# A hybrid GLA and mLSTM block on one core: TensorE's order in the heads written out by stages

## The chip, the core and the metric

The kernel runs on one core of a Trainium2 chip. The metric is the device time of one execution in microseconds (us). A core has five engines that run beside each other and are kept in step by semaphores: TensorE (PE in the profile; matrix products, with PEld for loading their weights), VectorE (DVE), ScalarE (ACT), GpSimd (POOL) and SyncE (SP, which issues the DMAs here). Each engine executes its own list of instructions in order.

## The reference

One layer of a backbone block: 512 latent tokens and 256 context tokens of width 2048, all in float32. After an RMSNorm with a shift and a scale, one input projection feeds two groups of four heads each. The first four heads are gated linear attention (GLA) with a decay for each channel, the last four are mLSTM with an exponential input gate. Each head has keys and queries of 128 and values of 256, runs in both directions, and each latent scan starts from the final context state of its direction.

```
rel = where(tril, bcum[j] - bcum[i], -inf)              # GLA, bcum = cumsum(log decay)
scores = einsum('jk,ik,jik->ji', q, k, exp(rel))
o = scores @ v + (q * exp(bcum)) @ s                    # s: state so far
s_new = exp(b_end) * s + (k * exp(b_end - bcum)).T @ v
```

Head outputs are normalised, gated and multiplied by an output matrix; then come a second RMSNorm, a SwiGLU mixer of width 5504 with a 3x3 depthwise convolution, and a final RMSNorm.

## The kernel before

Tiles have 128 partitions. Activations are kept transposed, the width in 16 tiles of 128 x 512. A product with float32 weights is made as three products of a faster format: each weight chunk is split into a high part (a cast on ScalarE, L89) and a low part (a subtraction on VectorE, L90), and mm3 multiplies high by high, high by low and low by high (all these products show as L95). `load_split` loads a chunk of two 128-row blocks through SP, splits it with high priority, and also takes `rate` items from a list of fillers: chunks of the modulation product, which are summed on VectorE, ScalarE and GpSimd (L228 to L235) and closed by small TensorE products.

The order of the work. Instructions are traced in Python, and a planner orders each engine's list by priority (order of tracing, with blocks raised by `high_priority`) and by its own estimate of when operands are ready. Instructions marked with `keep_in_program_order` stay in traced order among each other. `mm` does so while `pinned[0]` is set, which is the case in `project_first` alone, the stage ahead of the heads. In the heads TensorE's order is thus the planner's.

The heads. `project(h)` makes the products of head h into six PSUM banks (q, k, two of v, and two of the context's k and v), in eight chunks of six groups. `evict` copies them out (ScalarE and VectorE). Head 1's sums are made early, together with head 0's, so that head 1 needs no projection of its own. PSUM has six banks for projections and two (`psb`) for all the rest.

`gla` (heads 0 to 3) makes, in this order: the context's decays (cdec, a log-sigmoid of three ScalarE steps and one on VectorE, csum by triangles of ones, kd, and the context's state cst); the latent decays (dec, log-sigmoid, a scan bt for each direction at L589, and b2, the same across blocks, L593 and L596); the scores sd of a token with itself; nine levels, with blocks of 1 to 256 tokens; qi; the output products po (L662); and `finish`, which normalises and transposes (yt). In a level with block b, the decays of the tokens relative to the edge between two neighbour blocks are formed. GpSimd subtracts for the one side (L617, L618), VectorE for the other (L80), ScalarE takes the exponential of all (L621), VectorE multiplies by q and k (L83), TensorE multiplies (sl, L631 and L643), and VectorE copies the result under a mask (L634). The tile ex of a level has two buffers.

`ml_gates` is traced ahead of head 4 and makes the mLSTM gates for all heads: small products pre, a log-sigmoid, two scans for each direction, and transposes pa of the results. `mlstm` (heads 4 to 7) makes the context's state (kt, cst), exponentials of gate differences (pg, qs, ed, with a triangular mask on GpSimd), scores s, outputs po and `finish`. After the heads come the gate projections (ga), the output projection (wo) and the mixer.

Of the kernel before, what the change touches and what calls it, by code (L numbers as in the profile page):

```python
# [18 lines left out]
P = 128  # L19
# [50 lines left out]
def block_kernel(ctx: ExitStack, tc: tile.TileContext, a: dict, out: bass.AP):  # L70
# [27 lines left out]

    def mm3(o, ah, al, bh, bl, start, stop, **kw):
# [69 lines left out]
    def unit(src, name, xh, xl, n=4):  # L169

        accs = [acc(f"{name}_{i}") for i in range(n)]
# [111 lines left out]
    def project(h):  # L283

        banks = [acc(f"a{h}_{g}", BANKS[g]) for g in range(6)]
# [243 lines left out]
    def finish(h, ob, ssq, yT):  # L529

        var = wtile(f"var{h}", "st1", TJ)
        scr = wtile(f"scr{h}", "st2", TJ)
        r = wtile(f"rs{h}", "st3", TJ)
        mean_eps(var, ssq, DV)
        rsqrt(var, scr, r)
        for j in range(TJ):
            V.tensor_scalar(out=ob[:, j, :], in0=ob[:, j, :], scalar1=r[:, j : j + 1], scalar2=None, op0=ALU.mult)
        for b in range(2):
            ps = psb(f"yt{h}_{b}")
            for j in range(TJ):  # L540
                PE.transpose(ps[:, P * j : P * j + P], ob[:, j, P * b : P * b + P], ident)
# [4 lines left out]
    def gla(h, pair, qk, v, kn, vn, yT):  # L546
        wlr = wk.tile([17, 2, DK], F32, name=f"wlr{h}", tag="wlr")
        nc.sync.dma_start(wlr, a["w_lr"][h])

        cla = ytile(13, f"cla{h}", (P, 2, CJ, DK))  # L550
        ct = ytile(15, f"ct{h}", (P, 2, CJ, DK))
        for d in range(2):
            ps = psb(f"cdec{h}{d}", (P, CJ, DK))
            for j in range(CJ):
                PE.matmul(ps[:, j, :], glr[0:17, T + P * j : T + P * j + P], wlr[:, d, :], start=True, stop=True)
            log_sigmoid(cla[:, d], ps, ct[:, d])
        ps = psb(f"csum{h}", (P, 2, CJ, DK))
        for d in range(2):
            tri = cc(C_LS) if d == 0 else cc(C_US)
            for j in range(CJ):  # L560
                more = j == d
                PE.matmul(ps[:, d, j, :], tri, cla[:, d, j, :], start=True, stop=not more)
                if more:
                    PE.matmul(ps[:, d, j, :], ones, cla[:, d, 1 - j, :], start=False, stop=True)
        kd = ytile(14, f"kd{h}", (P, 2, CJ, DK))
        S.activation(kd, ps, AF.Exp, scale=DECAY)
        for j in range(CJ):
            mul(kd[:, :, j], kd[:, :, j], kn[j].unsqueeze(1).to_broadcast([P, 2, DK]))
        ps = psb(f"cst{h}", (P, 2, DV))
        for d in range(2):  # L570
            for j in range(CJ):
                PE.matmul(ps[:, d, :], kd[:, d, j, :], vn[j][:, 0:DV], start=(j == 0), stop=(j == CJ - 1))
        s0 = wtile(f"s0{h}", "state", 2, DV + 2)
        S.copy(s0[:, :, 0:DV], ps)

# [6 lines left out]
        for d in range(2):  # L582
            ps = psb(f"dec{h}{d}")
            PE.matmul(ps, wlr[:, d, :], glr[0:17, 0:T], start=True, stop=True)
# [4 lines left out]
            V.tensor_tensor_scan(out=o, data0=seg, data1=x, initial=0.0, op0=ALU.mult, op1=ALU.add)  # L589
        for d in range(2):  # L590
# [7 lines left out]


        sc = wtile(f"sc{h}", "la", 2, TJ, P)  # L600
        scd, sc1 = sc[:, 0], sc[:, 1]
        sc2 = [ytile(12 + i, f"sc2{h}{i}", (P, 2, 2 * P)) for i in range(2)]
        ps = psb(f"sd{h}", (P, TJ, P))
        for j in range(TJ):
            PE.matmul(ps[:, j, :], qk[1][:, P * j : P * j + P], qk[0][:, P * j : P * j + P], start=True, stop=True)
        V.scalar_tensor_tensor(out=scd, in0=ps, scalar=2.0, in1=ident.unsqueeze(1).to_broadcast([P, TJ, P]),
                               op0=ALU.mult, op1=ALU.mult)
        for lv, b in enumerate(LEVELS + [P, 2 * P]):
            src = bt if b < P else b2
            ex = wk2.tile([P, 2, T], F32, name=f"ex{h}_{lv}", tag="ex")  # L610
            e4 = ex.rearrange("p s (n a b) -> p s n a b", a=2, b=b)
            sf = src[0].rearrange("p (n a b) -> p n a b", a=2, b=b)
            sb = src[1].rearrange("p (n a b) -> p n a b", a=2, b=b)
            n = T // (2 * b)
            rf = sf[:, :, 0, b - 1 : b].to_broadcast([P, n, b])
            rb = sb[:, :, 1, 0:1].to_broadcast([P, n, b])
# [10 lines left out]
            if b <= P:  # L627
                ps = psb(f"sl{h}_{lv}", (P, TJ, P))
                for i in range(TJ):
                    j = i if b < P else i ^ 1  # L630
                    PE.matmul(ps[:, i, :], ex[:, 1, P * i : P * i + P], ex[:, 0, P * j : P * j + P],  # L631
                              start=True, stop=True)
# [4 lines left out]
            else:  # L637
                for half in range(2):
                    ps = psb(f"sl{h}_{lv}_{half}", (P, 2, 2 * P))
                    for ii in range(2):  # L640
                        i = 2 * half + ii
                        j0 = 2 * P * (1 - half)
                        PE.matmul(ps[:, ii, :], ex[:, 1, P * i : P * i + P], ex[:, 0, j0 : j0 + 2 * P],  # L643
                                  start=True, stop=True)
                    S.copy(sc2[half], ps)
        qi = wtile(f"qi{h}", "tmp", 2, T)
        for d in range(2):
            S.activation(qi[:, d, :], b2[d], AF.Exp, scale=DECAY)
        mul(qi, qi, qk[0].unsqueeze(1).to_broadcast([P, 2, T]))
# [3 lines left out]
        for j in range(TJ):  # L653
# [7 lines left out]
            for n, (l, r) in enumerate(parts):  # L661
                PE.matmul(po, l, r, start=(n == 0), stop=(n == len(parts) - 1))  # L662
            S.activation(junk, po, AF.Square, accum_out=ssq[:, j : j + 1])
            V.tensor_copy(ob[:, j, :], po)
        finish(h, ob, ssq, yT)

    def ml_gates():
# [11 lines left out]
        for t, r in ((0, li), (1, pf)):  # L679
            for c0, n, at in ((0, T, lat0), (T, TC, ctx0)):  # L680
                ps = psb(f"pre{t}{c0}", (36, n))
                for d in range(2):
                    e = C_ID + 32 + 8 * d + 4 * t
                    PE.matmul(ps[rows[d], :], cst[32:48, e : e + H], glr[32:48, c0 : c0 + n], start=True, stop=True)
# [16 lines left out]
        add(cum, cum, gmx)  # L701
        dg = wk.tile([36, H], F32, name="dg", tag="st1")
        for d in range(2):
            pa = psb(f"pa{d}", (P, CJ + 2 * TJ, H))
            e = cst[rows[d], C_ID + 32 * d : C_ID + 32 * d + H]
            for j in range(CJ + TJ):
                s = ctx0[d] + P * j if j < CJ else lat0[d] + P * (j - CJ)
                PE.transpose(pa[:, j, :], li[rows[d], s : s + P], e)
            for j in range(TJ):
                s = lat0[d] + P * j  # L710
                PE.transpose(pa[:, CJ + TJ + j, :], cum[rows[d], s : s + P], e)
# [7 lines left out]
            PE.matmul(pg, cst[rows[d], C_ONE : C_ONE + 1].to_broadcast([H, P]), dg[rows[d], :], start=True, stop=True)  # L719
            V.tensor_copy(gccol[:, d, :], pg)  # L720
        for d in range(2):
# [4 lines left out]
    def mlstm(h, _, qk, v, kn, vn, yT):  # L726
# [9 lines left out]
        for d in range(2):  # L736
            ps = psb(f"cst{h}{d}", (P, DV + 2))
            for j in range(CJ):
                PE.matmul(ps, kt[:, d, j, :], vn[j], start=(j == 0), stop=(j == CJ - 1))
            S.copy(c0[:, d, :], ps)  # L740

        qs = wtile(f"qs{h}", "tmp", 2, T)
        pd = []
        for d in range(2):
            rows = slice(32 * d, 32 * d + H)
            pg = psb(f"pg{h}{d}")
            PE.matmul(pg, cst[rows, C_ID + 32 * d + hh : C_ID + 32 * d + hh + 1].to_broadcast([H, P]), negg[rows, :],
# [16 lines left out]
            pd.append(spans)  # L764
        for i in range(TJ):
            ps = psb(f"s{h}{i}")
            PE.matmul(ps, k[:, P * i : P * i + P], q, start=True, stop=True)
            for d in range(2):
                e, j0, j1 = pd[d][i]
                mul(e, e, ps[:, j0:j1])  # L770
        ssq = wtile(f"ssq{h}", "ssq", TJ)
        junk = wtile(f"junk{h}", "kn", DV)
        ob = wtile(f"ob{h}", "la", TJ, DV)
        for j in range(TJ):
            for d in range(2):
                po = psb(f"po{h}_{j}{d}", (P, DV + 2))
                js = slice(P * j, P * j + P)
                PE.matmul(po, qs[:, d, js], c0[:, d, :], start=True, stop=False)
                rng = range(j + 1) if d == 0 else range(j, TJ)
                for i in rng:  # L780
                    e, j0, _ = pd[d][i]
                    PE.matmul(po, e[:, P * j - j0 : P * j - j0 + P], v[i], start=False, stop=(i == rng[-1]))  # L782
# [10 lines left out]
            S.activation(junk, ob[:, j, :], AF.Square, accum_out=ssq[:, j : j + 1])  # L793
        finish(h, ob, ssq, yT)

    yT = []
    mod_fillers((2, 3, 4), 3)
    for h in range(2 * H):
        if h == 1:
# [3 lines left out]
        else:  # L803
            tiles = evict(h, first if h == 0 else project(h))
        if h == H:
            ml_gates()
        (mlstm if h >= H else gla)(h, *tiles, yT)
# [8 lines left out]
    for g in range(4):  # L816
        accs = unit(a["w_gates"][g], f"ga{g}", *hx)
# [259 lines left out]
```

## Time and profile before

| what | value |
|---|---|
| median of 3 runs | 2632.07 us (2631.95 to 2634.08) |
| the profiled execution | 2632.04 us |
| its span in the trace | 2630.2 us |
| TensorE busy | 2557.7 us |
| the chain that ended last, TensorE's share | 85% |

The span runs from the first to the last instruction of the trace; 1.8 us of the execution lie around it. In the chain's list and the timelines, the columns are start, length and what ran; in the groups of instructions, busy time in us, mean length in ns, and the idle time of the engine ahead of them with what ended it. Products are pipelined, so a length of one product overlaps that of the next. The heads run from about 209 us to 836 us.

### The profile page before, as it was taken

To read this page: it belongs to the slowest core of one execution; us is meant where nothing else is said; L and a number is where in the kernel's file an instruction comes from. 1 tells how busy PE (TensorE), PEld (TensorE's weight loads), DVE (VectorE), ACT (ScalarE), POOL (GpSimd) and SP (SyncE) were. 2 spreads that over 40 slices of the span, in tenths; PEclk is the share of its full clock that TensorE was granted. 3 is DMA by queue.
4 is the path that set the end of the run, shared out by engine and by line. 5 is a ranking of instruction groups with operands and counts; after the bars stand their busy time and mean duration, and the time that the engine had idled before them with its cause. 6 is when DMAs were issued, how large, how long until landed. Compare 5 with 4: busy or idle time off the path is not lost.

```text
span 2630.2 us, 31995 instructions
## 1 busy us (share of the span) xinstructions
PE 2557.7 (97%) x12866; PEld 2137.8 (81%) x12866; DVE 1362.1 (52%) x1971; ACT 861.3 (33%) x1219; POOL 285.9 (11%) x255
## 2 busy tenths in 40 slices
PE   6999999899999999999999999999999999999998
PEld 4887888778987887887878888888888888888887
DVE  6656664654334455547676436543653365336534
ACT  4223443323333444334343223222322233223332
POOL 0002221302112232310231000000000000000001
PEclk9999999999999999999999999999999999999998
DMA  8750101213322566642554222222233223222333
GB/s 317 281 198 34 39 35 67 71 41 112 126 90 106 191 222 232 204 165 76 192 184 160 96 96 96 97 96 97 97 100 100 97 96 97 96 96 87 102 96 101
DMA packets 96348, 321.38 MB, mean 122 GB/s; under 512 B 10884, under 2 KB 15304, under 8 KB 96200
## 3 DMA queue, kind: packets, MB, share of 16 engines
q1 hardware_dynamic: 96200, 319.34, 35.2%
q8 instruction: 101, 1.65, 0.3%
q14 instruction: 47, 0.39, 0.0%
HBM read 315.10 MB, written 4.19 MB: 121 GB/s over the span
## 4 chain that ended last, share of the span: by engine, by line
PE 85%; DVE 7%; DMA 3%; ACT 2%; issue 2%; POOL 0%; SPq 0%; POOLq 0%; ACTq 0%; DVEq 0%
PE ug L95 17%; PE dn L95 17%; PE uv L95 16%; PE a L95 14%; PE wo L95 6%; PE ga L95 5%; DMA raw_m<-in_w_mod 2%; PE po L662 2%; PE po L782 1%; PE ps_m L95 1%; PE sl L631 1%; DVE cv L924 1%; DVE ex L80 1%; PE dl L95 1%; DVE ex L83 1%
## 5 line engine op out<-in xcount | busy, mean ns | idle before, releaser
L95 PE MATMUL ug<-h2h,hi_ug 128*128 128x512 f32 x688 | 269.0, 392 | 1.6 <-ACT h2h L883 1.6
L95 PE MATMUL uv<-h2h,lo_uv 128*128 128x512 f32 x688 | 268.7, 391 | 1.4 <-DVE lo_uv L90 1.4
L95 PE MATMUL uv<-h2h,hi_uv 128*128 128x512 f32 x688 | 268.4, 390 | 1.4 <-ACT hi_uv L89 1.4
L95 PE MATMUL ug<-h2h,lo_ug 128*128 128x512 f32 x688 | 268.8, 391 | 0.2 <-DVE lo_ug L90 0.2
L95 PE MATMUL ug<-h2l,hi_ug 128*128 128x512 f32 x688 | 268.7, 391 | 0.0
L95 PE MATMUL uv<-h2l,hi_uv 128*128 128x512 f32 x688 | 268.4, 390 | 0.0
L95 PE MATMUL dn<-gh,hi_d 128*128 128x512 f32 x644 | 250.5, 389 | 0.0
L95 PE MATMUL dn<-gl,hi_d 128*128 128x512 f32 x644 | 250.5, 389 | 0.0
L95 PE MATMUL dn<-gh,lo_d 128*128 128x512 f32 x644 | 250.5, 389 | 0.0
L924 DVE SCALAR_TENSOR_TENSOR cv<-pad,cwt,cv 128x512 f32<-128x512 f32 x344 | 242.3, 759 | 10.6 <-ACT cv L922 9.1
L233 POOL TENSOR_TENSOR sum_m<-sum_m,raw_m 128x512 f32<-128x512 f32 x112 | 173.8, 1551 | 550.8 <-ACT raw_m L232 315.0
L90 DVE TENSOR_TENSOR lo_ug<-raw_ug,hi_ug 128x1024 fp32r<-128x1024 f32 (+1 forms) x88 | 106.8, 1214 | 243.0 <-ACT hi_ug L89 243.0
L90 DVE TENSOR_TENSOR lo_uv<-raw_uv,hi_uv 128x1024 fp32r<-128x1024 f32 (+1 forms) x88 | 105.3, 1197 | 181.1 <-ACT hi_uv L89 180.7
L90 DVE TENSOR_TENSOR lo_d<-raw_d,hi_d 128x1024 fp32r<-128x1024 f32 x82 | 98.7, 1204 | 165.5 <-ACT hi_d L89 164.6
L231 DVE SCALAR_TENSOR_TENSOR sum_m<-raw_m,csil,sum_m 128x512 f32<-128x512 f32 x112 | 101.0, 902 | 152.0 <-DMA raw_m<-in_w_mod 148.5
L89 ACT CAST hi_ug<-raw_ug 128x1024 fp32r<-128x1024 f32 (+1 forms) x88 | 90.8, 1032 | 269.6 <-PE ug L95 202.0
L89 ACT CAST hi_d<-raw_d 128x1024 fp32r<-128x1024 f32 x82 | 85.1, 1037 | 278.7 <-PE dn L95 224.4
L89 ACT CAST hi_uv<-raw_uv 128x1024 fp32r<-128x1024 f32 (+1 forms) x88 | 90.9, 1033 | 251.5 <-PE uv L95 181.0
L95 PEld LDWEIGHTS uv<-h2h,lo_uv 128*128 128x128 f32 x688 | 129.5, 188 | 29.7 <-DVE lo_uv L90 2.7
L95 PEld LDWEIGHTS ug<-h2h,hi_ug 128*128 128x128 f32 x688 | 129.8, 189 | 28.7 <-ACT h2h L883 1.9
L95 PEld LDWEIGHTS uv<-h2h,hi_uv 128*128 128x128 f32 x688 | 129.6, 188 | 28.5 <-ACT hi_uv L89 1.8
L95 PEld LDWEIGHTS ug<-h2h,lo_ug 128*128 128x128 f32 x688 | 129.7, 189 | 27.9 <-DVE lo_ug L90 0.6
(310 smaller groups left out, 5279.2 us busy)
## 6 DMA issues: line engine op xcount, KB each, us to landing
raw_m<-in_w_mod SPq DMA_DIRECT2D x192, 512.0 KB, 4.4
raw_ug<-in_w_up SPq DMA_DIRECT2D x80, 512.0 KB, 3.1
raw_uv<-in_w_up SPq DMA_DIRECT2D x80, 512.0 KB, 3.2
raw_d<-in_w_down SPq DMA_DIRECT2D x79, 512.0 KB, 3.3
raw_h<-in_w_heads SPq DMA_DIRECT2D x64, 512.0 KB, 3.2
raw_ga<-in_w_gates SPq DMA_DIRECT2D x32, 512.0 KB, 3.3
raw_wo<-in_w_out SPq DMA_DIRECT2D x32, 512.0 KB, 4.1
xl<-in_xT SPq DMA_DIRECT2D x16, 256.0 KB, 5.3
```

Of the source, the lines that this page charges most:

```text
L80: V.tensor_tensor(out=o, in0=x, in1=y, op=ALU.subtract)
L83: V.tensor_tensor(out=o, in0=x, in1=y, op=ALU.mult)
L89: S.copy(hi, x)
L90: return V.tensor_tensor(out=lo, in0=x, in1=hi.bitcast(F32), op=ALU.subtract).ins
L95: ins = PE.matmul(*args, **kw)
L231: V.scalar_tensor_tensor(out=dv, in0=raw[:, 0, :], scalar=ce, in1=dv, op0=ALU.mult, op1=ALU.add)
L233: G.tensor_tensor(out=po, in0=po, in1=raw[:, 1, :], op=ALU.add)
L631: PE.matmul(ps[:, i, :], ex[:, 1, P * i : P * i + P], ex[:, 0, P * j : P * j + P], start=True, stop=True)
L662: PE.matmul(po, l, r, start=(n == 0), stop=(n == len(parts) - 1))
L782: PE.matmul(po, e[:, P * j - j0 : P * j - j0 + P], v[i], start=False, stop=(i == rng[-1]))
L924: V.scalar_tensor_tensor(out=t3, in0=src, scalar=w, in1=t3, op0=ALU.mult, op1=ALU.add)
```

## The change

It makes three edits, all in the heads.

TensorE's order is written out. `pinned` is set for all of the heads, and every product and transpose of the stages goes through `mm` or `tr`. The projection becomes a generator that yields after each group with the group's length; the stages (`gla`, `gla_prep`, `ml_gates`, `mlstm`) become generators that yield how much of the projection is to stand behind what they have just traced; `weave` runs the two together. While heads 0 and 1 run, the projection of head 2 is the fill; for every later head it is the next head's, and in head 7 the first unit of the gate projections. What is left of the projection follows after the head's stages.

The decays are made early. `gla_prep` holds the dec, cdec and csum stages. Head 0's are traced ahead of head 0, those of head h + 1 between head h's output products and its `finish`. The state cst and qi move behind the third level. `ml_gates` is traced behind head 3's `finish`.

The levels' differences are made by VectorE alone, one instruction for each direction over 512 elements, which writes both halves of ex crosswise; the exponential becomes two instructions, for the two signs. In the levels of 128 and 256 the subtraction is gone: ScalarE takes it as a bias (`ends`), in 8 and 4 instructions.

```diff
+    def weave(stages, steps):
+        debt = 0.0
+        for need in stages:
+            debt += need
+            while debt > 0:
+                took = next(steps, None)
+                if took is None:
+                    debt = 0.0
+                    break
+                debt -= took
...
+    def project_steps(h, banks):
         for kp in range(KP):
             rate[0] = 2 if h >= H and kp >= 3 else 0
             wh, wl = load_split(a["w_heads"][h, kp], f"h{h}_{kp}")
             for g in range(6):
                 project_chunk(kp, wh, wl, banks[g], g)
-        return banks
+                yield (1.36, 1.36, 1.44, 1.44, 1.04, 1.04)[g]
...
+    def gla_prep(h, out):
...
+            V.tensor_tensor_scan(out=o, data0=seg, data1=x, initial=0.0, op0=ALU.mult, op1=ALU.add)
+        yield 4
...
+            log_sigmoid(cla[:, d], ps, ct[:, d])
...
+        yield 3
+        ps = psb(f"csum{h}", (P, 2, CJ, DK))
...
+    def gla(h, pair, qk, v, kn, vn, yT, prep, fill, after):
...
+        yield fill
         for lv, b in enumerate(LEVELS + [P, 2 * P]):
...
-            G.tensor_tensor(out=e4[:, 0, :, 1, :], in0=sf[:, :, 1, :], in1=rf, op=ALU.subtract)
-            G.tensor_tensor(out=e4[:, 0, :, 0, :], in0=sb[:, :, 0, :], in1=rb, op=ALU.subtract)
-            sub(e4[:, 1, :, 0, :], rf, sf[:, :, 0, :])
-            sub(e4[:, 1, :, 1, :], rb, sb[:, :, 1, :])
-            S.activation(ex, ex, AF.Exp, scale=DECAY)
+            if b < P:
...
+                sub(crossed(ex, b, True), sf[:, :, ::-1, :], rf)
+                sub(crossed(ex, b, False), sb, rb)
+                S.activation(ex[:, 0, :], ex[:, 0, :], AF.Exp, scale=DECAY)
+                S.activation(ex[:, 1, :], ex[:, 1, :], AF.Exp, scale=-DECAY)
+            else:
...
+                            S.activation(ex[:, s, at : at + b], b2[d][:, at : at + b], AF.Exp,
+                                         scale=-DECAY if s else DECAY, bias=ends[:, s, d, e : e + 1])
...
+            yield fill
+            if lv == 2:
...
+                yield 1
...
-        finish(h, ob, ssq, yT)
+        if h + 1 < H:
+            yield from after
+            yield 1.4
+            finish(h, ob, ssq, yT)
+        else:
+            yield 5
+            finish(h, ob, ssq, yT)
+            yield from after
...
     def ml_gates():
...
+                yield 1
...
         add(cum, cum, gmx)
+        yield 16
...
+            yield 1.4
...
     mod_fillers((2, 3, 4), 3)
+    pinned[0] = True
+    preps = [{} for _ in range(H)]
+
+    def stages(h, tiles):
+
+        after = gla_prep(h + 1, preps[h + 1]) if h + 1 < H else ml_gates() if h + 1 == H else ()
+        if h < H:
+            yield from gla(h, *tiles, yT, preps[h], 2.4 if h < 2 else 4, after)
+        else:
+            yield from mlstm(h, *tiles, yT, after)
+
+    tiles = evict(0, first)
     for h in range(2 * H):
-        if h == 1:
+        if h != 1:
+            if h + 1 < 2 * H:
+                nxt = 2 if h == 0 else h + 1
+                accs = [acc(f"a{nxt}_{g}", BANKS[g]) for g in range(6)]
+                steps = project_steps(nxt, accs)
+            else:
+                rate[0] = 1.5
+                accs = [acc(f"ga0_{i}") for i in range(4)]
+                steps = unit_steps(a["w_gates"][0], "ga0", *hx, accs)
+        if h == 0:
+            weave(gla_prep(0, preps[0]), steps)
+        weave(stages(h, tiles), steps)
```

In `mlstm` the yields are 2.8 behind cst, 2.8 behind pg, 1.4 behind each of the four s, 1.4 behind each of the four pairs of po, and 4.2 ahead of `finish`.

More of the change, by code (lines that the diff above doesn't have):

```diff
@@ L167, in load_split, with unit_steps @@
         return hi, lo
-    def unit(src, name, xh, xl, n=4):
-        accs = [acc(f"{name}_{i}") for i in range(n)]
+    def unit_steps(src, name, xh, xl, accs):
+        n = len(accs)
         for kp in range(KP):
@@ L544, in finish @@
             S.activation(yT[-1], ps, AF.Copy, scale=gnh[:, g : g + 1])
-    def gla(h, pair, qk, v, kn, vn, yT):
-        wlr = wk.tile([17, 2, DK], F32, name=f"wlr{h}", tag="wlr")
+    def gla_prep(h, out):
+        wlr = wk2.tile([17, 2, DK], F32, name=f"wlr{h}", tag="wlr")
         nc.sync.dma_start(wlr, a["w_lr"][h])
[L550 to L574, printed above, removed]
         la = wtile(f"la{h}", "la", 2, T)
@@ L589, in gla @@
             V.tensor_tensor_scan(out=o, data0=seg, data1=x, initial=0.0, op0=ALU.mult, op1=ALU.add)
+        yield 4
+        cla = wtile(f"cla{h}", "cla", 2, CJ, DK)
+        ct = ytile(15, f"ct{h}", (P, 2, CJ, DK))
+        for d in range(2):
+            ps = psb(f"cdec{h}{d}", (P, CJ, DK))
+            for j in range(CJ):
+                mm(ps[:, j, :], glr[0:17, T + P * j : T + P * j + P], wlr[:, d, :], start=True, stop=True)
+            log_sigmoid(cla[:, d], ps, ct[:, d])
         for d in range(2):
@@ L597, in gla @@
                                 scalar1=b2[d][:, e : e + 1], scalar2=None, op0=ALU.add)
-        sc = wtile(f"sc{h}", "la", 2, TJ, P)
+        ends = wtile(f"ends{h}", "ends", 2, 2, 3)
+        for d in range(2):
+            src = b2[d][:, P - 1 : 3 * P : P] if d == 0 else b2[d][:, P : 3 * P + 1 : P]
+            for i, sgn in enumerate((-DECAY, DECAY)):
+                V.tensor_scalar(out=ends[:, i, d, :], in0=src, scalar1=sgn, scalar2=None, op0=ALU.mult)
+        yield 3
+        ps = psb(f"csum{h}", (P, 2, CJ, DK))
@@ new lines, in gla_prep, with crossed @@
+        for d in range(2):
+            tri = cc(C_LS) if d == 0 else cc(C_US)
+            for j in range(CJ):
+                more = j == d
+                mm(ps[:, d, j, :], tri, cla[:, d, j, :], start=True, stop=not more)
+                if more:
+                    mm(ps[:, d, j, :], ones, cla[:, d, 1 - j, :], start=False, stop=True)
+        kd = ytile(14, f"kd{h}", (P, 2, CJ, DK))
+        S.activation(kd, ps, AF.Exp, scale=DECAY)
+        out.update(bt=bt, b2=b2, kd=kd, ends=ends)
+    def crossed(ex, b, fwd):
+        n = T // (2 * b)
+        at, step = (b, T - b) if fwd else (0, T + b)
+        return bass.AP(ex.tensor, ex.offset + at, [ex.ap[0], [2 * b, n], [step, 2], [1, b]])
@@ L683, in ml_gates @@
                     e = C_ID + 32 + 8 * d + 4 * t
-                    PE.matmul(ps[rows[d], :], cst[32:48, e : e + H], glr[32:48, c0 : c0 + n], start=True, stop=True)
+                    mm(ps[rows[d], :], cst[32:48, e : e + H], glr[32:48, c0 : c0 + n], start=True, stop=True)
                 for d in range(2):
@@ L718, in ml_gates @@
             pg = psb(f"pgc{d}", (P, H))
-            PE.matmul(pg, cst[rows[d], C_ONE : C_ONE + 1].to_broadcast([H, P]), dg[rows[d], :], start=True, stop=True)
+            mm(pg, cst[rows[d], C_ONE : C_ONE + 1].to_broadcast([H, P]), dg[rows[d], :], start=True, stop=True)
             V.tensor_copy(gccol[:, d, :], pg)
+            yield 1.4
         for d in range(2):
@@ L803, in block_kernel @@
         else:
[L804 to L807, printed above, removed]
+            for _ in steps:
+                pass
+            if h + 1 < 2 * H:
+                tiles = evict(h + 1, accs)
+    pinned[0] = False
     st_2.close()
```

85 lines of the change are left out of this document (56 added, 29 removed).

## The prediction

> **What bounds the kernel now.** I read the engine table of the page, then the table by stages for the stretch that the change rewrites (the eight heads, from 209 us on), then what TensorE waited for there, then the chain of waits in single heads. TensorE is the bound:
>
> ```profile
> PE 2557.7 (97%) x12866; PEld 2137.8 (81%) x12866; DVE 1362.1 (52%) x1971; ACT 861.3 (33%) x1219; POOL 285.9 (11%) x255
> ```
>
> The other engines are far from full, so the time can only change where TensorE stands still or runs slowly. The stages, in their order, are heads 0, 1, 2 and 3 (GLA), the mLSTM gates, and then heads 4 to 6 with most of the start of head 7. The columns are the stretch, its length, busy time of each engine, and the granted TensorE clock.
>
> ```profile
> core 0: us, PE busy (x) PEld busy (x) DVE busy (x) ACT busy (x) POOL busy (x), PEclk, DMA share, GB/s
> 209.00:285.00 76.00, 72.45 (x423) 62.61 (x424) 45.02 (x78) 30.46 (x55) 13.69 (x18) 0.98 0.08 29
> 285.00:356.00 71.00, 67.65 (x401) 58.11 (x400) 45.13 (x84) 29.66 (x50) 14.99 (x18) 1.00 0.11 38
> 356.00:422.00 66.00, 61.90 (x357) 54.48 (x358) 40.79 (x66) 24.03 (x38) 14.94 (x18) 0.97 0.10 33
> 422.00:514.00 92.00, 82.97 (x493) 73.40 (x492) 57.79 (x85) 35.65 (x59) 32.17 (x29) 0.98 0.25 86
> 514.00:556.00 42.00, 40.94 (x248) 35.16 (x246) 17.80 (x21) 10.89 (x15) 0.45 (x1) 1.00 0.17 62
> 556.00:804.00 248.00, 246.04 (x1382) 214.22 (x1383) 102.40 (x232) 80.21 (x151) 42.26 (x48) 0.99 0.28 98
> ```
>
> TensorE idles 3.55 + 3.35 + 4.10 + 9.03 = 20.0 us in the GLA heads, 1.1 us in the gates, and 2.0 us in the mLSTM heads: 23.1 us. Nearly all of it in the GLA heads is one wait, the score product of a level waiting for VectorE's last factor (total, times, longest):
>
> ```profile
> PE sl L631 <- DVE ex L83: 17.0, 16, 3.4
> ```
>
> There is a second loss, in the clock. (1 - clock) x length is 1.5 + 2.0 + 1.8 + 2.5 = 7.8 us; I take 7, since part of it falls on idle time. These three rows show where it comes from: the same eight products, after 2.15, 2.34 and 3.37 us of idleness (in brackets), take 1.13, 1.52 and 2.08 us.
>
> ```profile
> 303.30 1.13 PE L631 MATMUL sl<-ex 128*128 128x128 f32 x8 [2.15 <-ACT hi_h L89]
> ...
> 373.38 1.52 PE L631 MATMUL sl<-ex 128*128 128x128 f32 x8 [2.34 <-DVE ex L83]
> ...
> 463.29 2.08 PE L631 MATMUL sl<-ex 128*128 128x128 f32 x8 [3.37 <-DVE ex L83]
> ```
>
> So some 30 us (23.1 + 7) are to be had, 1.1% of the time, and no more: the products themselves stay the same in number and shape.
>
> **The change: what it takes away.** In the heads TensorE now follows the written order: each stage, then a dose of the next head's projection. The dose is 2.4 (heads 0, 1) or 4 (heads 2, 3) per level. These numbers are times; a projection is 61.44 by them, and the trace agrees: 384 products at 34.14/212 are 61.8 us.
>
> ```profile
> 600.54 34.14 PE a L95 x212
> ```
>
> The waits between levels shrink if VectorE keeps pace. Its work per level now, from the groups of heads 0 to 3 (min/median/max in ns; then count, busy us, mean ns):
>
> ```profile
> L80 DVE TENSOR_TENSOR ex<-bt x56: 399/414/1485, 230.3 to 484.8; 128x256 f32<-128x256 f32 x56
> L83 DVE TENSOR_TENSOR ex<-ex,qk x27: 1202/1214/2299, 232.8 to 495.5; 128x1024 f32<-128x1024 f32 x27
> L83 DVE TENSOR_TENSOR ex<-ex,e x18: 667/682/1141, 301.9 to 330.6; 128x512 f32<-128x512 f32 x18
> ```
>
> ```profile
> L634 DVE COPY_PREDICATED sc<-msk,sl 128x512 f32<-128x512 uint8 x28 | 20.6, 736 | 4.6 <-PE sl L631 4.5
> L90 DVE TENSOR_TENSOR lo_h<-raw_h,hi_h 128x1024 fp32r<-128x1024 f32 x20 | 25.4, 1271 | 23.7 <-ACT hi_h L89 23.7
> ...
> L231 DVE SCALAR_TENSOR_TENSOR sum_m<-raw_m,csil,sum_m 128x512 f32<-128x512 f32 x7 | 6.6, 941 | 2.2 <-DMA raw_m<-in_w_mod 2.2
> ```
>
> GpSimd's two subtractions of 256 move to VectorE, merged with its own: it will do two of 512 instead of two of 256. A 512-wide two-input operation is 0.68 us in its median. The maxima of 1.5 to 2.3 us are what the same operations took at worst with GpSimd's subtractions beside them; those go. So a level costs VectorE 2 x 0.68 + 1.21 + 0.74 = 3.3 us of durations, or 3.0 us once neighbours overlap by 0.08 us (four subtractions of 0.41 us take 1.34 us in a row):
>
> ```profile
> 230.42 1.34 DVE ex L80 x4
> ```
>
> The weight split comes on top, 1.27 us per 7.68 of dose: 0.4 us in a level of 2.4, 0.66 us in a level of 4. TensorE spends 1.1 us on the eight products and the dose: 3.5 us per level in heads 0 and 1 against 3.4 on VectorE, 5.1 against 3.7 in heads 2 and 3. Head 3 also carries ten of the modulation fillers from half-way on (0.94 us each on VectorE, about one per level): 4.6 against 5.1. Levels of 128 and 256 lose their subtractions to ScalarE's bias; it was busy 24 to 36 us of 66 to 92, so that hides.
>
> What I leave standing in the levels: the first level of head 0, whose decays have only a dose of 7 ahead of them, 1 us (0 to 3); the pace of heads 0 and 1, 16 waits of 0.3 us, 5 us (0 to 10: nothing if the 0.1 us of slack holds, 10 if VectorE also sits idle for ScalarE's cast ahead of each split, 23.7/20 = 1.2 us by the row above); head 2, 1 us (0 to 3); head 3, 2.5 us (1 to 7, of the 9.0 now). Sum 9.5 us.
>
> **What it adds: stretches without fill.** The doses are finite, and I counted them step by step. Head 0 takes its own 7 plus 33.4, and 20.3 of the second projection are left for head 1, which asks for 33.4. They end exactly after level 64. From there on head 1 is bare: levels 128 and 256, the output products, the decays of head 2 and the transposes. Before, the third projection filled this place. Levels and output products follow each other closely (0.5 us lost), but the decays are a chain through ScalarE and VectorE:
>
> ```profile
> 218.91 1.06 PE dec L584 x2
> ...
> 222.30 0.70 DVE la L527
> 223.03 1.22 DVE bt L589
> 224.25 0.58 DVE la L527
> ```
>
> From the start of dec to the end of the second la are 5.9 us; the second cdec needs that PSUM bank. Its log-sigmoid is three ScalarE steps and one VectorE step:
>
> ```profile
> L526 ACT ACTIVATE ct<-ct 128x256 f32<-128x256 f32 x8 | 3.2, 417 | 0.1
> ```
>
> ```profile
> L527 DVE SCALAR_TENSOR_TENSOR cla<-cdec,ct 128x256 f32<-128x256 f32 x8 | 3.3, 422 | 8.1 <-ACT ct L526 8.1
> ```
>
> That is 4 x 0.42 = 1.7 us, 2.2 with cdec itself (0.5) ahead; the sums by triangle (1.4 us of products) end near 9.5 us. TensorE's own work in it is 4 us, so 5.5 us stand idle: 6 us with the 0.5 (4 to 8).
>
> The second bare stretch is at the gates. Head 3 with its output, finish and four gate products asks for 50; 11.2 of the projection's 61.44 are left after the last of them, for a stage that asks for 16. The chain there now:
>
> ```profile
> 543.44 0.98 PE pre L684 x4
> ...
> 549.72 0.96 DVE pf L527
> 550.74 1.64 issue
> 552.38 1.19 DVE lo_h L90
> 553.60 1.76 DVE cum L693
> 555.38 0.96 DVE li L80
> ```
>
> From the last pre's end (544.4) to li's end (556.3) are 11.9 us; two more scans of 1.7 us and a sum of 0.96 us follow before the transposes of cum, at 16.3 us, or 15.1 without the split in between. The fill ends at 11.2, the transposes of li take 0.4: 4 us idle. Then transposes, pgc, the four subtractions, the exponential, kt and the first product of head 4 follow one another with about 2.6 us idle, and 0.9 us for head 4's late eviction: 7.5 us (5 to 10), where 1.1 stand now.
>
> Third, heads 5 to 7 begin with cst straight behind the last chunk of their own projection. Today a chunk lies between the halves:
>
> ```profile
> 634.68 0.95 PE cst L739 x4
> 635.63 2.05 PE a L95 x9
> 637.68 0.87 PE cst L739 x4
> ```
>
> Without it, TensorE waits for the eviction of kn and for kt, about 1.3 us after the last product; with 0.4 us more for ScalarE's exponentials behind pg, 1.7 us per head, 5 us (2 to 8; the upper end is a split that stands in VectorE's queue ahead of kt). For these waits what is queued behind on TensorE is everything, since its order is fixed; DMA issues on SP are the same in number (the wlr loads come one head earlier, and have two buffers), and no transfer is late for them.
>
> Last, the clock: these idle stretches will cost it too. One drop at head 1's tail and two at the gates, at 1.7 us each (head 3's row above loses 0.02 x 92 = 1.8 us with one such wait, head 2's 2.0), are 5 us (2 to 7).
>
> The Trainium skill, "TensorE: Matmul & The Clock Gate", Part 1, states that the clock falls to a half only after a whole idle window of about 3.4 us. By that rule head 1's tail, whose single waits stay under 3 us, would cost nothing, and the sum would be 1.7 to 3 us lower. The trace differs: 2.34 us of idleness were enough for slow products (1.52 us), though 2.15 were not.
>
> **The sum.** Taken away 30 us; put back 9.5 + 6 + 7.5 + 5 + 5 = 33 us. Net +3 us. The profiled execution took 2632.04 us (span 2630.2 and 1.8 around it), the median of the runs is 2632.07: 2635 us.
>
> **The rivals.** (a) VectorE keeps pace and the level waits vanish: the first group falls from 9.5 to 1, and the starts of heads 5 to 7 and the clock cost 1 to 2 us less each. Net -9: 2623 us. For it: 0.1 us of slack in heads 0 and 1, over 1 us in head 2, no GpSimd beside it. Against: VectorE's 23.7 us of waiting for the cast. (b) Slower: VectorE's queue, which is in order too, stands behind a weight split that waits for its cast, and VectorE becomes the bound of the levels. The point from which it decides is 3.5 us per level in heads 0 and 1 (5.1 in head 3); with half of the 1.2 us of each wait and a split's full length in every other level it is some 4.2 us, and costs 16 x 0.7 = 11 us, 6 more than I put, in head 3 its upper end (4 more) and ahead of kt 2 more: net +15, 2647 us. (c) The order changes little, because the planner had already laid chunks between the levels, and the waits only change their place: 2632 us. Beside it stands the result of the clock rule, by which a wait under 3.4 us costs no clock, 2632 to 2633 us as well; the skill's page is the one named above.
>
> **How the numbers follow.** Forecast 0.38, (a) 0.27, (b) 0.25, (c) with the clock rule 0.10. A measurement of this kernel can tell 0.2%, 5.3 us, from no change. The forecast's own range, 2629 to 2641, lies for 0.25 within that, 0.11 slower, 0.02 faster; (a) is faster but for 0.01; (b) slower; (c) no change. So faster 0.28, same 0.36, slower 0.36. All lower ends together would give 2616 us, all upper ends 2658; I leave out a tenth at each side: 2618 to 2652.
>
> **What would show it.** Right: TensorE's idle time in the GLA levels falls from 17 us to under 8; two new idle places, ahead of cdec and csum after head 1's output products and ahead of pa after the gates; idle time before cst in heads 5 to 7; a granted clock below 1 in just these slices. Wrong: a wait of sl on VectorE at nearly every level of heads 0 and 1 (that is (b)), or a full TensorE in the bare stretches. A change of more than 2 us outside the heads, in the output projection's start, would be something I have not priced.

## The result, and the profile after

The changed kernel takes 2636.86 us (median of 20 runs, 2633.72 to 2640.02) against 2633.30 us for the kernel before in the same runs: a ratio of 1.0013, with a 95% interval of 1.0007 to 1.0020. The profiled execution took 2634.89 us, its span is 2633.2 us. The forecast was 2635 us, no change to speak of. The sum was right; two of its terms were far off in opposite directions, and the prediction did not see that what the change gains does not need TensorE's order to be fixed.

The engine table of the changed kernel's page, first row:

```profile
PE 2552.0 (97%) x12866; PEld 2140.2 (81%) x12866; DVE 1352.4 (51%) x1971; ACT 870.3 (33%) x1287; POOL 223.8 (8%) x183
```

The table by stages, cut at the changed kernel's own bounds: head 0, head 1, heads 2 and 3 (from their sd), the gates, heads 4 to 6 with the start of head 7. The columns are as before.

```profile
209.00:289.00 80.00, 77.40 (x443) 67.55 (x444) 54.75 (x102) 38.45 (x83) 0.00 (x0) 0.96 0.10 34
289.00:349.00 60.00, 52.86 (x302) 45.99 (x301) 42.17 (x80) 30.36 (x66) 0.00 (x0) 0.90 0.08 27
349.00:441.00 92.00, 90.95 (x555) 82.36 (x554) 49.50 (x79) 36.62 (x73) 0.79 (x1) 0.99 0.12 41
441.00:512.00 71.00, 69.77 (x434) 64.14 (x432) 39.22 (x57) 26.40 (x52) 12.74 (x10) 1.00 0.32 104
512.00:541.00 29.00, 22.04 (x136) 17.21 (x136) 21.93 (x34) 8.57 (x17) 0.37 (x1) 0.90 0.17 55
541.00:808.00 267.00, 257.61 (x1444) 226.86 (x1445) 95.97 (x224) 81.85 (x150) 43.59 (x48) 0.98 0.29 95
```

TensorE idles 2.6 + 7.1 + 1.1 + 1.2 + 7.0 + 9.4 = 28.4 us, where it was 23.1. The idle time has moved: heads 2 and 3 are full, the end of head 1, the gates and the mLSTM heads are not. The clock is low in these places, and in head 0 as well (0.96), where TensorE hardly idles. What TensorE waited for in the heads (total, times, longest):

```profile
PE cst L95 <- DVE kt L795: 7.8, 4, 2.2
PE yt L100 <- DVE ob L560: 5.3, 2, 2.9
PE pa L100 <- DVE cum L86: 4.1, 1, 4.1
PE s L95 <- ACT ed L822: 2.9, 4, 0.8
PE cdec L95 <- DVE la L550: 2.6, 2, 1.9
PE csum L95 <- DVE cla L550: 2.1, 3, 1.0
PE dec L95 <- DVE glr L514: 2.1, 2, 1.6
PE sl L95 <- DVE ex L83: 1.8, 3, 0.8
```

The wait that led the list before, sl for VectorE's factor, is down from 17.0 us to 1.8 us. Seven others now stand above it.

For an account of the whole I took every TensorE record from the first glr product to the first product of the second gate unit (662.6 us before, 666.3 after), and compared its distance to the next start with the distance that the fastest third of its own kind shows. The excess before idle gaps rose by 6.8 us (30.4 to 37.2), the excess inside stretches of half clock by 4.9 (7.8 to 12.7), and all small losses between products, which the prediction did not price, fell by 8.1 (16.6 to 8.5). That makes +3.6 us, the whole difference. The last of the three depends on how the kinds are drawn: with other choices the same records give changes of +7 to +8, +5 to +6 and -9 to -10 us, so its fall is shown, its level is not. The plain windows say the same: from 208.9 us to the second gate unit TensorE's busy time falls from 636.59 us (the row below) to 632.93 us (its row stands beside that of the planner's order, further down), although its clock is lower.

```profile
208.90:869.30 660.40, 636.59 (x3577) 548.49 (x3578) 341.56 (x633) 237.75 (x414) 134.09 (x147) 0.99 0.22 76
```

### The profile page after: what moved, and what is told of

Read it like the earlier page. It is cut to its first block, busy times and chain, and to the rows that moved or that the text cites. A ratio compares the mean times of both kernels' runs of the same rounds, so it can differ in the third digit from the quotient of the medians.

```text
span 2633.2 us, 31946 instructions
## 1 busy us (share of the span) xinstructions
PE 2552.0 (97%) x12866; PEld 2140.2 (81%) x12866; DVE 1352.4 (51%) x1971; ACT 870.3 (33%) x1287; POOL 223.8 (8%) x183
## 4 chain that ended last, share of the span: by engine, by line
PE 87%; DVE 5%; DMA 4%; ACT 2%; issue 2%; POOL 1%; SPq 0%; POOLq 0%; DVEq 0%; ACTq 0%
PE ug L95 17%; PE dn L95 17%; PE uv L95 16%; PE a L95 16%; PE wo L95 6%; PE ga L95 5%; PE po L95 3%; DMA raw_m<-in_w_mod 3%; PE ps_m L95 1%; PE sl L95 1%; DVE cv L1018 1%; PE dl L95 1%; DMA raw_h<-in_w_heads 1%; PE cst L95 1%; PE s L95 1%
```

## The experiments

In the stated expectations, theory A carries the prediction further: the written order cures the level waits, and the stretches without fill are its price. (The prediction itself did not divide the cure between the order and the new differences.) All ratios are to the kernel before, which ran beside each experiment; a difference in us to the changed kernel is one of medians, and the median of the kernel before moved by 1.1 us between the experiments.

**Filling the bare stretches.** Three edits, first one by one. For the first two the fill became one generator, which evicts the finished projection and goes on with the next, where the head allows it (`junk` has a buffer of its own):

```diff
+    def run_on(n):
+        while n < 2 * H:
+            accs = [acc(f"a{n}_{g}", BANKS[g]) for g in range(6)]
+            yield from project_steps(n, accs)
+            while not cross[0]:
+                yield None
+            done[n] = evict(n, accs)
+            yield 0.0
+            n += 1
...
     for h in range(2 * H):
+        cross[0] = h in (1,)
```

> The changed kernel, but when the second projection's products run out in head 1, head 2's tiles are evicted at once and the third projection goes on as fill. Theory A (the change trades the waits between levels for stretches without fill, and pays the clock for them): the 6.2 us of idle time from 289 to 349 us and about 4 us of half clock behind it go, so the time falls by 8 to 10 us from the changed kernel: ratio to the kernel before 0.997 to 0.9985. Rival B (the waits only move, because the chains on ScalarE and VectorE set the pace of the heads): the time falls by 2 us or less, ratio 1.000 to 1.001, and new waits stand at the first levels of head 2.

Measured: 2634.17 us, 1.0006 (0.9997 to 1.0015). Theory A fails here. The two stages from 289 us on, in the table by stages of this run:

```profile
289.00:349.00 60.00, 58.68 (x352) 51.73 (x352) 36.94 (x60) 27.56 (x61) 0.00 (x0) 1.00 0.10 34
349.00:441.00 92.00, 85.55 (x516) 76.94 (x515) 57.12 (x105) 40.37 (x81) 2.99 (x3) 0.96 0.17 58
```

Head 1's place is full now: 1.3 us idle at a full clock, against 7.1 at 0.90. But from 349 to 441 us TensorE idles 6.45 us where it idled 1.05. Of this, 1.34 us are head 1's own transposes, which now fall behind 349 us, and 4.39 us are head 2's:

```profile
438.18 2.02 PE L100 MATMUL yt<-cst,ob 128*128 128x128 f32 x8 [4.39 <-DVE ob L560]
```

The third projection, drawn on by head 1, ends at 432 us. Head 2's decays are still covered by it, its transposes are not. So the wait moved after all, yet not to where rival B had it (the first levels of head 2; sl waits 0.9 us in all): it moved because fill is a budget.

The second edit is the same with `h in (3,)`, for the gates:

> The changed kernel, but when the fourth projection's products run out at the gates behind head 3, head 4's tiles are evicted at once and the next projection goes on as fill. Theory A: the 7 us idle at the gates and 1 to 2 us of half clock go: 7 to 9 us less than the changed kernel, ratio to before 0.998 to 0.9995. Rival B: 2 us or less, ratio 1.000 to 1.001, with the wait for the gates standing at head 4's first product instead.

Measured: 2627.34 us, 0.9981 (0.9972 to 0.9989), 9.5 us below the changed kernel. Theory A holds: heads 4 to 7 have products to spare (21 of 61.44 are asked for), so nothing runs short later.

The third puts two groups ahead of the context's state products:

```diff
     def mlstm(h, _, qk, v, kn, vn, yT, after):
...
+        yield 2.72
         c0 = wtile(f"c0{h}", "state", 2, DV + 2)
```

> The changed kernel, but heads 4 to 7 put two groups of the next projection ahead of the context's state products, behind the scaling kt on VectorE. Theory A: the 7.8 us that these products wait for kt, and the two half-clock stretches behind them in heads 5 to 7 (2.8 us), go: 8 to 10 us less than the changed kernel, ratio 0.997 to 0.9985. Rival B: the wait moves on to the scores behind the exponentials of pg, since ScalarE and VectorE start no earlier: 2 us or less, ratio 1.000 to 1.001.

Measured: 2625.12 us, 0.9965 (0.9952 to 0.9979), 11.7 us below the changed kernel, 2 more than expected. TensorE's waits from 618 to 860 us, in the changed kernel and then in this one:

```profile
PE cst L95 <- DVE kt L795: 6.5, 3, 2.2
PE yt L100 <- DVE ob L560: 2.4, 1, 2.4
PE s L95 <- ACT ed L822: 2.1, 3, 0.8
PE po L95 <- DVE ob L856: 0.5, 2, 0.3
```

```profile
PE yt L100 <- DVE ob L560: 3.0, 2, 2.0
PE po L95 <- ACT ob L855: 1.7, 1, 1.7
PE po L95 <- DVE ob L857: 0.6, 1, 0.6
```

The wait for kt is gone, and so is the wait of s for ScalarE's exponentials: the groups now fall otherwise, and in head 5 three of them lie between pg and s where one lay.

> The three together, and the third projection may run out at the end of head 2 as well. Theory A: the three gains add up: 20 to 26 us less than the changed kernel, ratio to before 0.9915 to 0.994; TensorE idles under 10 us from 207 us to the second gate unit, and its clock falls at most twice there. Rival B: 6 us or less, ratio 0.999 or more.

Measured: 2621.78 us, 0.9953 (0.9940 to 0.9966). The three are worth 15 us together, less than the two good ones alone (9.5 + 11.7), and between the two forecasts (20 to 26 us, and 6 or less). TensorE still idles 17.8 us in the heads, 10.0 of them in one wait:

```profile
208.90:856.50 647.60, 629.82 (x3576) 549.54 (x3577) 332.40 (x633) 246.81 (x481) 70.74 (x75) 0.98 0.23 78
```

```profile
PE yt L100 <- DVE ob L560: 10.0, 5, 3.0
```

So the bare stretches that the prediction counted are a part of the price, not all of it.

**Which of the three edits does what.** The changed kernel with the differences of before:

```diff
...
+            src = bt if b < P else b2
...
+            G.tensor_tensor(out=e4[:, 0, :, 1, :], in0=sf[:, :, 1, :], in1=rf, op=ALU.subtract)
+            G.tensor_tensor(out=e4[:, 0, :, 0, :], in0=sb[:, :, 0, :], in1=rb, op=ALU.subtract)
+            sub(e4[:, 1, :, 0, :], rf, sf[:, :, 0, :])
+            sub(e4[:, 1, :, 1, :], rb, sb[:, :, 1, :])
+            S.activation(ex, ex, AF.Exp, scale=DECAY)
```

> The changed kernel with the levels' differences as before: GpSimd subtracts for one side and VectorE for the other, one exponential for all, also in the levels of 128 and 256. Order and doses stay. Theory A (the written order cures the level waits): the score products wait for VectorE 2 to 8 us in all, the time is within 6 us of the changed kernel, ratio to before 1.000 to 1.004. Rival C (taking GpSimd out of the levels cures them): the waits of the score products come back, 12 us or more, and the time is 10 us or more above the changed kernel, ratio above 1.005.

Measured: 2644.41 us, 1.0043 (1.0028 to 1.0058): 7.5 us above the changed kernel, between the two forecasts, and its wait for the levels is in the range that theory A gave, though this run has the early decays as well as the written order:

```profile
PE sl L95 <- DVE ex L83: 5.6, 6, 1.8
```

The mirror image is the kernel before with the new differences alone (its L650 is the product's line):

> The kernel before with the levels' differences alone changed: VectorE alone, one instruction for each direction, the bias in the levels of 128 and 256; TensorE's order stays the planner's. Theory A: the score products still wait 12 to 20 us for VectorE, ratio 0.998 to 1.002. Rival C: these waits fall under 6 us and the kernel is faster than before by 8 to 15 us, ratio 0.994 to 0.997.

Measured: 2619.20 us, 0.9945 (0.9930 to 0.9961). This is rival C's time: the third edit alone gains 14 us. The level waits fall from 17.0 to 9.2 us, which is not as far as rival C had it:

```profile
PE sl L650 <- DVE ex L83: 9.2, 8, 2.7
```

Then the changed kernel with the order left to the planner, one line less:

```diff
     mod_fillers((2, 3, 4), 3)
-    pinned[0] = True
     preps = [{} for _ in range(H)]
```

> The changed kernel without the fixed order: the planner may move TensorE's products in the heads, the traced order and all else stay. Theory A: the planner fills the bare stretches of head 1 and of the gates only as far as tiles allow, and misplaces products between levels again: level waits of 8 us or more, ratio 0.998 to 1.004. Rival (the fixed order is the whole loss): no bare stretches, level waits as short as in the changed kernel, ratio 0.992 to 0.996.

Measured: 2610.97 us, 0.9918 (0.9895 to 0.9942). Theory A falls: with TensorE's order not fixed, and the projection still traced between the stages, the change gains 22 us, and that one line costs 26. The planner lays the third projection's products into head 1's end, where the changed kernel's written order has none, and has no level wait left to speak of. The whole of the heads in this run, then the changed kernel (from 208.9 us to the second gate unit):

```profile
208.90:845.90 637.00, 626.97 (x3576) 546.79 (x3577) 330.33 (x634) 248.88 (x482) 70.39 (x75) 0.99 0.24 79
```

```profile
208.90:873.60 664.70, 632.93 (x3576) 552.55 (x3577) 332.41 (x634) 247.73 (x483) 70.54 (x75) 0.97 0.23 76
```

The same products, 10.0 us idle against 31.8. The other 6.0 us are busy time, with a clock of 0.99 against 0.97: 13.65 us at half clock here, 37.5 in the changed kernel. Its longest wait of all, and its only one for the levels:

```profile
PE pa L100 <- DVE cum L86: 3.0, 1, 3.0
...
PE sl L95 <- DVE ex L83: 0.3, 1, 0.3
```

The second edit by itself (traced by stages, decays early, differences as before, order left to the planner) is the fourth corner:

> The changed kernel without the fixed order and with the levels' differences as before: what is left is the early decays, the state products behind the third level and the traced order by stages. If the differences are worth 14 us beside any order (2633.6 to 2619.2 alone), this is 14 us above the changed kernel without the fixed order, some 2625 us, ratio 0.996 to 0.998, with 5 to 10 us of level waits. If the early decays are the gain by themselves, and both cure the same waits: 2612 to 2617 us, ratio 0.991 to 0.994.

Measured: 2612.01 us, 0.9920 (0.9907 to 0.9932): the second forecast. The early decays and the traced order bring 20 us without VectorE's differences, and 22 with them, which the intervals do not tell apart. Both lessen the same wait, which was 17.0 us before:

```profile
PE sl L95 <- DVE ex L83: 4.8, 7, 1.5
```

**Where the fixed order costs.** It was fixed in one half of the heads at a time, with `pinned[0] = h < H` and `pinned[0] = h >= H` at the top of the loop:

> The changed kernel with TensorE's order fixed in heads 0 to 3 and the gates, and left to the planner in heads 4 to 7. By the traces of the two whole versions, idle time and clock in heads 4 to 7 are 19 us with the fixed order and some 7 without: 12 us less than the changed kernel, some 2625 us, ratio 0.996 to 0.998. If the planner's freedom must span both (it needs the early heads to get ahead), 4 us less or nothing, ratio 0.9995 to 1.0015.

> The mirror image: TensorE's order left to the planner in heads 0 to 3 and the gates, fixed in heads 4 to 7. If the two losses add up: 14 us less than the changed kernel, some 2623 us, ratio 0.995 to 0.997, with cst waiting 6 to 8 us for kt as in the changed kernel. If they do not: 2630 us or more, ratio 0.9985 or more.

Measured: 2622.25 us, 0.9960 (0.9947 to 0.9973), and 2621.53 us, 0.9960 (0.9946 to 0.9974). Each half given free saves about 15 us, some 3 us more than forecast for the first and 1 for the second, and 30 us together against the 26 of both: within the intervals the losses add up. In the second the wait of cst for kt is 7.8 us, as in the changed kernel.

**The dose.**

```diff
-            yield from gla(h, *tiles, yT, preps[h], 2.4 if h < 2 else 4, after)
+            yield from gla(h, *tiles, yT, preps[h], 1.6 if h < 2 else 4, after)
```

> The changed kernel with doses of 1.6 in place of 2.4 behind the stages of heads 0 and 1, so that 15 us of the second projection are left over for head 1's last levels and decays. If a level costs VectorE 3.4 us, as forecast: TensorE would take 2.7 us per level, and the score products of heads 0 and 1 wait 0.7 us in 14 levels, 10 us, against 6 us saved behind head 1's output products: ratio to before 1.001 to 1.004. If VectorE's queue takes less than 2.8 us per level (a reserve that the forecast denied): waits of 2 us or less, and 5 to 10 us gained: ratio 0.997 to 0.999.

Measured: 2636.54 us, 1.0011 (1.0001 to 1.0021). The first forecast holds, and the second falls: fill saved in the levels is wanted there.

```profile
PE sl L95 <- DVE ex L83: 7.9, 6, 2.1
```

With 2.7 us per level for TensorE, six waits for VectorE appear, up to 2.1 us; with 3.5 us heads 0 and 1 had two, up to 0.7. That agrees with the price of 3.4 us per level on VectorE. The time itself stays that of the changed kernel (1.0013), at the lower end of the first forecast.

**A version that beats both.** The three refills of above without the fixed order:

> The kernel of the three refills (head 1's tail, the gates, the groups ahead of the state products) without the fixed order: the planner orders TensorE in the heads. Theory now (the fixed order is the loss, the early decays and VectorE's differences are the gains): the planner fills all that the tiles leave free, and the earlier eviction leaves more free at the gates: at or below the changed kernel without the fixed order, ratio to before 0.988 to 0.992, idle time from 207 us to the second gate unit under 12 us. Rival (refills only help a fixed order; the planner's own choice is already as full): the same as without them, 0.9905 to 0.993.

Measured: 2610.46 us, 0.9917 (0.9905 to 0.9930). It is 22 us faster than the kernel before, but no faster than the planner's order without the refills (0.9918). The ratio lies in the ranges of both forecasts; that it is no lower than without the refills is the rival's: no gain is shown for them in an order that is not fixed. Its trace idles more than that of the run without them (12.8 us of 642.70 against 10.0 of 637.00), but the two profiled executions differ as well: 2614.90 us here, the slowest of five, and 2608.92 there. So the idle time cannot be set against the medians.

```profile
208.90:851.60 642.70, 629.93 (x3576) 550.61 (x3577) 331.10 (x634) 247.49 (x482) 72.73 (x75) 0.98 0.24 78
```

## Why the prediction was right or wrong

- **The bound and what could be had** (TensorE; 23 us idle, 7 of clock): right. The planner's version of the change took 22 us of it. Outside the heads the spans before and after differ by 1.3 us, less than the 2 us that the prediction set as a sign.
- **The waits between levels** (9.5 us left, of 20): too high, sl waits 1.8 us. VectorE's price of 3.4 us per level was right, as the smaller dose shows; wrong was to add 0.3 us for each level on top, and 2.5 us for head 3's fillers. Rival (b), VectorE as the bound, thereby fell; rival (a) had this term right, at 1 us, and fell by the others.
- **Head 1's bare end** (6 us): right in place and size, 7.1 us less 0.9 of sl. Its make-up was other than described. The forecast chain of cdec and csum cost 2.9 us, and 2.9 us more were a wait that it did not have: the transposes yt for VectorE's scaling. VectorE's list in the changed kernel shows why.

```profile
343.42 0.15 DVE L83 TENSOR_TENSOR scr<-rs 128x4 f32<-128x4 f32 x1
343.49 1.07 DVE L80 TENSOR_TENSOR ex<-bt 128x512 f32<-128x512 f32 x1
344.40 0.16 DVE L83 TENSOR_TENSOR scr<-scr,var 128x4 f32<-128x4 f32 x1
344.46 1.22 DVE L83 TENSOR_TENSOR qi<-qi,qk 128x1024 f32<-128x1024 f32 x1
345.59 0.16 DVE L150 TENSOR_SCALAR scr<-scr 128x4 f32<-128x4 f32 x1
345.66 1.06 DVE L80 TENSOR_TENSOR ex<-bt 128x512 f32<-128x512 f32 x1
346.56 0.16 DVE L83 TENSOR_TENSOR rs<-rs,scr 128x4 f32<-128x4 f32 x1
346.62 0.41 DVE L83 TENSOR_TENSOR kd<-kd,kn 128x256 f32<-128x256 f32 x1
346.95 1.13 DVE L560 TENSOR_SCALAR ob<-ob,rs 128x256 f32<-128x256 f32 x4
```

  Between the small steps of head 1's finish (0.16 us each) the planner put three large ones of head 2 (1.07, 1.22 and 1.06 us), which the early decays had made ready. TensorE's next product hung on the small ones. In the run with all refills the same wait, yt for ob, adds up to 10.0 us, in heads 1, 2, 4 and 7; that it has this cause is shown for head 1 alone.
- **The gates** (7.5 us): right, 7.0 us, and borne out by the refill, which gains 9.5 us with the clock.
- **The starts of heads 5 to 7** (5 us, up to 8): mis-sized. kt alone takes 2.2 us per head, 6.5 us, and s another 2.1: 8.6 us, above the upper end. In two rows of the changed kernel's timeline the state product stops after two of its eight records:

```profile
626.79 0.67 PE L95 MATMUL cst<-vn,kt 128*128 128x258 f32 x2
629.64 2.00 PE L95 MATMUL cst<-vn,kt 128*128 128x258 f32 x6 [2.18 <-DVE kt L795]
```

- **The clock** (5 us): mis-sized the most. (1 - clock) x length over the stages is 3.2 + 6.0 + 0.9 + 0 + 2.9 + 5.3 = 18.3 us, against 7.8 before by the same measure. Part of it falls on idle time; on products it is 12.7 us by the account above. The prediction counted three drops of 1.7 us, at head 1's end and the gates. The trace has 37.5 us at half clock: 13.65 us at head 1's end, 10.2 at the gates, 3.4 each at the starts of heads 5 and 7, and twice 3.4 in head 0. The two in head 0 contradict the sign that the clock would be below 1 in just the idle slices.
- **What was not priced**: 8.1 us of small losses between products. They hid the error of the clock. The forecast of idle time, 9.5 + 6 + 7.5 + 5 = 28 us, meets the 28.4 measured in the same way: the levels idle 7.7 us less, the starts of heads 5 to 7 some 3.6 more, and about 5 us lie where none was forecast, above all ahead of dec in head 0 (1.6) and of csum in heads 0 and 2 (0.7 and 1.0). So it was luck that the sum came within 1 us of the measured change. The mechanism was the one that it named: bare stretches and the clock take back what the levels give.
- **What the gain came from**: not seen. By the prediction's terms the change takes away 30 - 9.5 = 20.5 us, and its stretches without fill, with the clock, add 6 + 7.5 + 5 + 5 = 23.5. The runs come near to both: 22 us gained without the fixed order, 26 lost by it. But the prediction tied the two together, as if the gain were the written order's, and has no rival in which the planner, given the other two edits, does better; (c) has it that the order changes little. The runs show two edits that shorten the level waits under the planner's own order: VectorE's differences (9.2 us left of 17.0) and the early decays with the traced order (4.8). That fixing the order shortens them as well is not shown: with the early decays and the old differences they are 5.6 us with the order fixed and 4.8 without, and no run fixes the order alone. Its price uses up the gain of the others. How much of the second edit's 20 us is the early decays and how much the mere order of tracing, which is the planner's priority, stays open: no run had one without the other.

The Trainium skill, "TensorE: Matmul & The Clock Gate", Part 1, has the clock fall after a whole idle window of about 3.4 us. Here it does not take so much: no gap in head 1's end was longer than 2.9 us, and the clock was halved for all of this stretch, in which TensorE was busy 65% of the time by the profile. Ahead of the drops at 630.65 and 804.73 us TensorE was busy 1.23 and 1.37 us of the 3.41 us before.

```profile
337.10:350.75 13.65, 8.85 (x34) 7.38 (x35) 12.83 (x33) 8.16 (x18) 0.00 (x0) 0.50 0.00 0
```

## What to carry to other kernels

A wait can have several cures, and the cheapest one should be tried alone: here making the levels' differences on VectorE alone gave 14 us, starting the next head's work early, with the stages traced in that order, 20 us, and fixing the order on top took all of it back. An order written out by hand fixes the good places and the bad ones alike: in this kernel every stage whose fill had run out, and every product that stood straight behind what it waits for, became idle time that the planner had mostly filled. Fill is a budget: count it to the end of the next stage too, since what is put into one gap is missing in another.

## What the runs showed of the hardware

TensorE's clock also fell without any idle gap. In the changed kernel four decay products of head 1 with 17 of 128 rows follow head 0's output products, at 273.13 us; from 275.66 to 279.07 us the granted clock is 0.50, with TensorE busy throughout:

```profile
275.66:279.07 3.41, 3.41 (x18) 3.41 (x17) 2.48 (x5) 2.08 (x5) 0.00 (x0) 0.50 0.02 5
```

A drop of this kind, beginning between 274.9 and 278.5 us, stands in six of the experiments (smaller dose, the first refill, GpSimd's differences, early decays alone, the last version, the order fixed for heads 4 to 7). It is missing in four others in which the same four products take the same 2.27 us from 272.87, 274.34, 273.59 and 274.12 us (the gates' refill, kt, all three refills, the order fixed for heads 0 to 3). So the narrow products alone do not decide it. Where they lie does, in these eleven traces. In each trace the stretches at half clock in the heads last 3.41 us or a whole multiple of it, and all of them lie on one grid of 3.41 us. In the seven traces with the drop the four products lie whole within one step of this grid, 2.24 us of it, and the clock is halved in the next step. In the four without it the grid cuts them, and no step holds more than 1.81 us of them. The rows below give the time of these four products alone, first the step ahead of the drop in the changed kernel, then the two steps that share them in the run with the order fixed for heads 0 to 3; the 0.58 behind is their weights' loading.

```profile
272.25:275.66 3.41, 2.24 (x4) 0.58 (x4) 0.00 (x0) 0.80 (x2) 1.00 0.00 0
```

```profile
272.55:275.96 3.41, 1.81 (x4) 0.58 (x4) 0.00 (x0) 0.60 (x1) 1.00 0.00 0
275.96:279.38 3.42, 0.43 (x2) 0.00 (x0) 0.69 (x1) 0.59 (x1) 1.00 0.00 0
```

That it is the 17 rows that count so little is an inference: no run changes their width.
